# Moving the lambda sums and the scaling of the last norm's factors in a two-layer decoder trunk on one Trainium2 core

## The chip, the core and the metric

The kernel runs on one NeuronCore of a Trainium2 chip. TensorE (PE in the profile, with PEld for its weight loads) multiplies; VectorE (DVE), ScalarE (ACT) and GpSimd (POOL) work elementwise; SyncE (SP) and, for some transfers, POOL and ACT issue DMAs. Each engine takes its own instructions strictly in order, and engines wait for one another through semaphores. The metric is the device time of one launch in microseconds (us), the median of several runs.

## What is computed

The input is 256 tokens of width 1024, in float32. Two layers follow, and each has three blocks with a LayerNorm behind every one: a SwiGLU feed-forward block, a mixer (a gated spatial unit beside differential attention), and a second feed-forward block. Cut to what the change touches:

```python
def _swiglu(x, w1, w3, w2):
    return (jax.nn.silu(x @ w1) * (x @ w3)) @ w2          # w2: 2816 x 1024

    lam_full = (jnp.exp(jnp.sum(lf[0] * lf[1])) - jnp.exp(jnp.sum(lf[2] * lf[3])) + lam_init)
    a = p[:, :, 0] - lam * p[:, :, 1]                     # in the attention of each layer

    for l in range(DEPTH):
        h = _swiglu(x, ffn_w1[l, 0], ffn_w3[l, 0], ffn_w2[l, 0])
        x = _layernorm(ALPHA * x + 0.5 * h, ln_g[l, 0], ln_b[l, 0])
        h = _mixer(x, l, ...)
        x = _layernorm(ALPHA * x + h, ln_g[l, 1], ln_b[l, 1])
        h = _swiglu(x, ffn_w1[l, 1], ffn_w3[l, 1], ffn_w2[l, 1])
        x = _layernorm(ALPHA * x + 0.5 * h, ln_g[l, 2], ln_b[l, 2])
```

The lambda of a layer is one number made from 256 inputs. It is wanted first in the attention of the first mixer. `ln_g[1, 2]` are the factors of the very last norm.

## The kernel before

**Precision and pieces.** Every operand is split into a high part in a reduced float32 format and a low part that holds the rest, and each product is three matmuls: high by high, low by high, high by low. A weight comes from memory into a tile `raw` of 128x2048 (or two tiles `home` of 128x1024). ScalarE copies 128x1024 of it to `whi` (line 195 in `stream`, line 247 in `split`), VectorE subtracts that from the raw values into `wlo` (lines 197 and 249), and TensorE uses both. A `whi` with its `wlo` is called a piece here. There are 4 raw tiles, and 8 tiles each for high and low parts; a tile is filled again when its last reader is done.

**The product with w2.** `gemm_seven` (line 380) runs four times, once for each feed-forward block; these four stretches of the program are called the four w2 stages. It takes part of the product by seven block products in place of eight, and for that sums of weight blocks are made on the chip. `r1` holds block w11, `r2` is w12 and `r3` is w22, both in home tiles. `plus` (line 356, its addition is line 359) makes r1 + r2, and later in the same tile (r1 + r2) + r3; `pieces` (line 362) splits each sum, then r3, then r2. `product` (line 372) is 12 matmuls (line 376) with one such sum, and `between` (line 415) puts a piece of the ordinary product, 12 matmuls of line 405, between two of them. So TensorE's order in a w2 stage is fixed: product, piece, product, piece and so on. After each block product `Norm.fold` (line 606, its instruction is line 609) adds its result from PSUM to the tokens on VectorE. `gather` (line 350) lets POOL's DMA queue add a further weight block onto a tile in place. At the end a list `held` of seven pieces is multiplied for one half of the tokens and then for the other.

**What sets the order.** TensorE's order is as written. The other engines' order comes from a scheduler, which works by priority and by edges. `behind(ins)` makes an edge: what is issued inside comes after `ins` on its engine. While `line[2]` is set, `inline` notes the latest high split of ScalarE in `line[0]` and the latest operation of the split stream of VectorE in `line[1]`, so that splits and sums stay in one line. Small work is put beside the stream with `beside(task, delay)` (line 137): `beat(w)` (line 124) advances a clock as matmuls are written, a block product by 1 and a `between` by 1, and a task runs on when the clock has passed its time. A `yield 22` in a task hands back until the clock is 22 further.

**Lambda.** `setup` (line 543) is such a task. It is started in the first block, by the first row of a late piece of the first products. It loads the small constants through POOL's queue, yields 22, and then does: halving of a gate bias (`gbh`, line 556), two multiplications for lambda (`lampr`, line 560), scaling of `dgs` (line 570, one for each layer), the sums (`ls`, a reduction on VectorE, line 562), the Exp of the sums (ScalarE, line 563, with a load of the activation table ahead of it), and lambda itself (`neg_lam`, line 566, one for each layer). `lam` and `lampr` are tiles of a ring of four.

**The last norm.** `Norm.__init__` loads the factors g and the offsets b of its norm, spread over 128 partitions, with `bc_load` (a DMA of POOL's queue, line 576). For the last norm ScalarE multiplies g by -0.5 in place at once (line 595, `bc<-bc`). g is first read in `Norm.part` at line 620.

Of the kernel before, what the change touches and what calls it, by code (L numbers as in the profile page):

```python
# [16 lines left out]
AF = mybir.ActivationFunctionType  # L17
# [32 lines left out]
def lambda_init(layer):  # L50
    return 0.8 - 0.6 * math.exp(-0.3 * layer)
# [3 lines left out]
def trunk(ctx, tc, x, xT, w13a, w13b, w2, wb, wqk, wu, wg, wgr, wbr, wbrr, wo, gateb, gatebr, sgug, sgub, sguwT, sgubias, lam, diffg,  # L55
          lng, lnb, lngT, lnbT, cosT, sinT, out):
    nc = tc.nc
    V, A, G, PE = nc.vector, nc.scalar, nc.gpsimd, nc.tensor
# [15 lines left out]
    def name(s):  # L74
        serial[0] += 1
        return f"{s}_{serial[0]}"
# [24 lines left out]
    def s512(s, n=4):  # L101
        return tmp.tile([P, 512], F32, tag="side", name=name(s), bufs=n)

    def sm(s, n, dtype=F32, bufs=2):
        return small.tile([P, n], dtype, tag=f"{s}{n}", name=name(s), bufs=bufs)
# [31 lines left out]
    def beside(task, delay):  # L137
        tasks.append([clock[0] + delay, task])
# [9 lines left out]
    line = [None, None, False]  # L148
# [6 lines left out]
    def behind(ins):  # L155

        return tc.issue_after(ins) if ins is not None else nullcontext()
# [189 lines left out]
    def halved(v):  # L347
        return v if isinstance(v, list) else [v[:, o : o + HC] for o in range(0, CH, HC)]
# [194 lines left out]
    def setup(after):  # L543
        G.memset(mask[:, :P], 0.0)
        make_causal_mask(nc, mask[:, P:], NEG)
        lam_t = s512("lam").rearrange("p (l f d) -> p l f d", l=DEPTH, f=4)
        for dst, src in ((x_tok[0], x[:P, :]), (x_tok[1], x[P:, :]), (cos_t, cosT), (sin_t, sinT), (dgs, diffg),
                         (gbh, gateb), (ln_g, lngT), (ln_b, lnbT), (lam_t, lam.partition_broadcast(P))):
            first = dst
            while len(first.shape) > 2:  # L550
                first = first[:, 0]
            V.tensor_copy(first[:, :1], after)
            G.dma_start(dst, src)
        yield 22
        with behind(added[0]):
            V.tensor_scalar(out=gbh, in0=gbh, scalar1=0.5, scalar2=None, op0=ALU.mult)
        pr = s512("lampr").rearrange("p (l f d) -> p l f d", l=DEPTH, f=4)[:, :, :2]
        for j in range(2):
            with behind(added[0]):
                V.tensor_tensor(out=pr[:, :, j], in0=lam_t[:, :, 2 * j], in1=lam_t[:, :, 2 * j + 1], op=ALU.mult)  # L560
        ls = const.tile([P, DEPTH, 2], F32, name="ls")
        V.tensor_reduce(out=ls, in_=pr, op=ALU.add, axis=AX.X)
        A.activation(ls, ls, AF.Exp)
        for l in range(DEPTH):
            nl = const.tile([P, 1], F32, name=f"neg_lam{l}")
            V.tensor_scalar(out=nl, in0=ls[:, l, 1:2], scalar1=ls[:, l, 0:1], scalar2=-lambda_init(l),
                            op0=ALU.subtract, op1=ALU.add)
            neg_lam.append(nl)
            with behind(added[0]):
                V.tensor_scalar(out=dgs[:, l : l + 1], in0=dgs[:, l : l + 1], scalar1=1.0 - lambda_init(l),  # L570
                                scalar2=None, op0=ALU.mult)

    def bc_load(src, after):
        t = res.tile([P, D], F32, tag="bc", name=name("bc"), bufs=2)
        V.tensor_copy(t[:, :1], after)
        spread[0] = G.dma_start(t, src.partition_broadcast(P)).ins
        return t

    class Norm:
# [6 lines left out]
        def __init__(self, l, i, scale, eps, after, last=False):  # L586
            self.scale, self.eps, self.last, self.done, self.front = scale, eps, last, set(), i
            self.ends, self.xhi, self.xlo, self.rows = [None] * NT, {}, {}, {}
            self.gT, self.bT = (v[:, l, i] for v in (ln_g, ln_b))
            self.y = x_tok  # L590
            self.group = 256 if last else 512
            self.st = [sm("st", D // self.group * 6, bufs=2) for _ in range(NT)]
            self.g, self.b = bc_load(lng[l, i], after), bc_load(lnb[l, i], after)
            if last:
                A.activation(self.g, self.g, AF.Copy, scale=-0.5)
                self.minus = s512("minus")
                A.activation(self.minus[:, :P], ident, AF.Copy, scale=-1.0)
                self.eps_t = self.minus[:, 2 * P : 2 * P + 1]
                V.memset(self.eps_t, eps)
                with behind(silu[0]):  # L600
                    A.activation(sm("first", 1), mask[:, :1], AF.Sqrt)
            else:
                self.via = []
                self.x = [xs.tile([P, 4, 512], F32R, tag="x", name=name("x")) for _ in range(2)]

        def fold(self, t, c, ps, op, first):

            y = self.y[t][:, c * 512 : (c + 1) * 512]
            V.scalar_tensor_tensor(out=y, in0=y, scalar=self.scale if first else 1.0, in1=ps, op0=ALU.mult, op1=op)
# [137 lines left out]
    def ffn(l, f, i, norm, last=False):  # L747
# [14 lines left out]
        def front(n, wait):  # L762

            tiles = {}

            def gate_(t, ps):
                pool, tag = ((act, "val"), (res, "bc"))[n in (1, NB - 1)]
                p = pool.tile([P, D], F32, tag=tag, name=name("planes"), bufs=2).rearrange("p (w c) -> p w c", w=2)
                tiles[t] = p
                with behind(norm.xhi[1, 0] if norm and (n, t) == (0, 0) else None):  # L770
                    silu[0] = A.activation(p[:, 1], ps, AF.Silu).ins

            def done(t, ps):
                p = tiles[t]
                s = p[:, 1]
                added[0] = V.tensor_tensor(out=s, in0=s, in1=ps, op=ALU.mult).ins
                beside(turned(n, t, s, p[:, 0], wait[t]), 0)
                if norm is None and (n, t) == (2, 0):
                    beside(setup(s[:, :1]), 0)
            return gate_, done  # L780
# [546 lines left out]
```

## Time and profile before

| what | value |
|---|---|
| median of 3 runs | 1192.87 us (1192.68 to 1193.38) |
| the profiled execution: time | 1193.55 us |
| its span, first to last instruction | 1191.8 us |
| TensorE busy | 1182.0 us (99%), 5771 matmuls |
| VectorE busy | 1012.0 us (85%) |
| ScalarE busy | 827.5 us (69%) |
| POOL busy | 291.3 us (24%) |
| read from HBM | 249.10 MB |

The four w2 stages begin at 124.65, 537.51, 712.51 and 1124.03 us of the span. The rows shown below come from views of the one profiled execution. A row of a timeline gives the start, the duration, the engine, the line, the operation, what it writes and reads, and how many instructions of one kind were merged; in brackets stands how long the engine sat idle before it and what ended that. Starts and durations are in us. Line numbers are those of the kernel before.

### The profile page before, as it was taken

To read this page: it belongs to the slowest core of one execution; us is meant where nothing else is said; L and a number is where in the kernel's file an instruction comes from. 1 tells how busy PE (TensorE), PEld (TensorE's weight loads), DVE (VectorE), ACT (ScalarE), POOL (GpSimd) and SP (SyncE) were. 2 spreads that over 40 slices of the span, in tenths; PEclk is the share of its full clock that TensorE was granted. 3 is DMA by queue.
4 is the path that set the end of the run, shared out by engine and by line. 5 is a ranking of instruction groups with operands and counts; after the bars stand their busy time and mean duration, and the time that the engine had idled before them with its cause. 6 is when DMAs were issued, how large, how long until landed. Compare 5 with 4: busy or idle time off the path is not lost.

```text
span 1191.8 us, 16673 instructions
## 1 busy us (share of the span) xinstructions
PE 1182.0 (99%) x5771; PEld 993.3 (83%) x5771; DVE 1012.0 (85%) x1558; ACT 827.5 (69%) x1418; POOL 291.3 (24%) x356
## 2 busy tenths in 40 slices
PE   9999999999999999999999999999999999999998
PEld 7888888888888888888888888888888888888877
DVE  6889989888688989889899889788965989988885
ACT  6688658559955677876567876666788556679751
POOL 1111301247420220051020161004464012102500
PEclk9999999999999999999999999999999999999999
DMA  9869975758855658699667699586675764886971
GB/s 352 273 206 265 293 272 203 265 190 230 245 203 183 223 182 274 195 294 265 217 221 263 195 294 272 178 303 221 219 207 194 252 193 153 277 246 216 280 217 36
DMA packets 129797, 276.15 MB, mean 232 GB/s; under 512 B 89088, under 2 KB 90160, under 8 KB 105648
## 3 DMA queue, kind: packets, MB, share of 16 engines
q1 hardware_dynamic: 121968, 248.80, 62.9%
q0 software_dynamic: 7312, 25.76, 9.2%
q8 instruction: 45, 0.74, 0.2%
q10 hardware_dynamic: 432, 0.52, 0.1%
q14 instruction: 40, 0.33, 0.1%
HBM read 249.10 MB, written 1.05 MB: 210 GB/s over the span
## 4 chain that ended last, share of the span: by engine, by line
PE 96%; DVE 2%; DMA 1%; issue 1%; SPq 0%; ACT 0%; ACTq 0%; DVEq 0%
PE bank L283 46%; PE bank L295 15%; PE sbank L376 11%; PE bank L405 9%; PE bank L302 7%; PE sbank L405 3%; PE bank L516 1%; PE sbank L986 1%; DMA raw<-in_w13b 1%; PE bank L376 1%; PE sbank L1042 1%; PE sbank L1160 1%; DVE wlo L249 1%; PE sbank L1040 0%; DVE raw L359 0%
## 5 line engine op out<-in xcount | busy, mean ns | idle before, releaser
L197 DVE TENSOR_TENSOR wlo<-raw,whi 128x1024 fp32r<-128x1024 f32 (+1 forms) x374 | 414.1, 1132 | 56.1 <-ACT whi L195 43.1
L195 ACT ACTIVATE whi<-raw 128x1024 fp32r<-128x1024 f32 (+1 forms) x378 | 352.8, 959 | 131.2 <-PE bank L283 44.2
L283 PE MATMUL bank<-whi,x 128*128 128x512 f32 x1224 | 386.4, 390 | 0.0
L283 PEld LDWEIGHTS bank<-whi,x 128*128 128x128 f32 x1224 | 229.8, 188 | 47.6
L283 PE MATMUL bank<-wlo,x 128*128 128x512 f32 x612 | 238.2, 389 | 0.0
L295 PE MATMUL bank<-x,whi 128*128 128x512 f32 x640 | 153.3, 391 | 0.0
L295 PEld LDWEIGHTS bank<-x,whi 128*128 128x128 f32 x640 | 118.2, 188 | 23.8
L283 PEld LDWEIGHTS bank<-wlo,x 128*128 128x128 f32 x612 | 114.9, 188 | 23.4
L249 DVE TENSOR_TENSOR wlo<-raw,whi 128x1024 fp32r<-128x1024 f32 (+1 forms) x96 | 110.6, 1169 | 19.7 <-ACT whi L247 10.8
L247 ACT ACTIVATE whi<-raw 128x1024 fp32r<-128x1024 f32 (+1 forms) x96 | 92.6, 982 | 35.6 <-DVE raw L359 20.9
L229 POOL COPY seven<-seven 128x512 uint16<-128x512 uint16 x16 | 58.0, 3678 | 112.9 <-ACT whi L195 54.6
L302 PEld LDWEIGHTS bank<-x,wlo 128*128 128x128 f32 x640 | 81.4, 191 | 2.9
L302 PE MATMUL bank<-x,wlo 128*128 128x256 f32 x640 | 82.6, 283 | 0.0
L405 PE MATMUL bank<-whi,hhi 128*128 128x512 f32 (+1 forms) x182 | 68.2, 375 | 0.0
L405 PE MATMUL bank<-whi,hlo 128*128 128x512 f32 (+1 forms) x182 | 67.9, 373 | 0.0
L405 PE MATMUL bank<-wlo,hhi 128*128 128x512 f32 (+1 forms) x182 | 67.9, 373 | 0.0
L962 POOL TENSOR_TENSOR swap<-swap,sin_t 128x512 f32<-128x512 f32 x16 | 28.1, 1759 | 101.4 <-DMA swap<-z 84.6
L723 POOL COPY nvia<-ntwo 128x256 uint16<-128x256 uint16 x20 | 9.5, 520 | 157.5 <-DMA ntwo<-nvia 94.2
L303 ACT ACTIVATE r<-bank 128x256 f32<-128x256 f32 x96 | 34.8, 371 | 16.7 <-PE bank L302 16.7
L359 DVE TENSOR_TENSOR raw<-raw,home 128x1024 f32<-128x1024 f32 x32 | 38.6, 1216 | 4.3 <-DMA home<-in_w13b 4.3
L376 PE MATMUL sbank<-whi,xhs 128*128 128x512 f32 x128 | 42.0, 389 | 0.0
L405 PEld LDWEIGHTS bank<-whi,hlo 128*128 128x128 f32 x182 | 34.3, 188 | 6.1
(283 smaller groups left out, 2153.4 us busy)
## 6 DMA issues: line engine op xcount, KB each, us to landing
raw<-in_w13b SPq DMA_DIRECT2D x68, 1024.0 KB, 5.5
raw<-in_w SPq DMA_DIRECT2D x32, 1024.0 KB, 6.0
raw<-in_wb SPq DMA_DIRECT2D x16, 1024.0 KB, 5.3
raw<-in_wqk SPq DMA_DIRECT2D x16, 1024.0 KB, 5.7
home<-in_w13b SPq DMA_DIRECT2D x16, 512.0 KB, 6.1
raw<-in_w13a SPq DMA_DIRECT2D x8, 1024.0 KB, 4.8
home<-in_w SPq DMA_DIRECT2D x16, 512.0 KB, 5.1
raw<-in_wgr SPq DMA_DIRECT2D x8, 1024.0 KB, 5.3
```

What stands on the lines that cost most here:

```text
L195: inline(A, A.activation(h, r, AF.Copy).ins)
L197: low = eng.tensor_tensor(out=w, in0=r, in1=h.bitcast(F32), op=ALU.subtract).ins
L229: eng.tensor_copy(out=o, in_=i)
L247: a = A.activation(hi, src, AF.Copy).ins
L249: return a, eng.tensor_tensor(out=lo, in0=src, in1=hi.bitcast(F32), op=ALU.subtract).ins
L283: PE.matmul(ps, xx, w, start=start and n == 0, stop=stop and n == 2)
L295: PE.matmul(b[-1], hi[:, k * P : (k + 1) * P], xc(k), start=k == 0, stop=False)
L302: PE.matmul(b[n][:, :T], lo[:, k * P : (k + 1) * P], xc(k)[:, :T], start=False, stop=k == KT - 1)
L303: emptied[0] = A.activation(r[:, s], b[n][:, T:], AF.Copy, scale=scale).ins
L359: inline(V, V.tensor_tensor(out=v, in0=v, in1=m, op=ALU.add).ins)
L376: PE.matmul(ps, x[o](k), y, start=start and k == n == 0, stop=stop and k == 3 and n == 2, skip_group_check=True)
L405: PE.matmul(q[c][t][:, :n] if o == 0 else more[:, :n], x(k, t), y, start=k == 8 and m == 0 and (c, t) != (1, 0), stop=k == FT - 1 and m == ...
```

## The change

```diff
@@ -551,7 +551,7 @@
-        yield 22
+        yield 33
         with behind(added[0]):
             V.tensor_scalar(out=gbh, in0=gbh, scalar1=0.5, scalar2=None, op0=ALU.mult)
@@ -592,7 +592,7 @@
             if last:
-                A.activation(self.g, self.g, AF.Copy, scale=-0.5)
+                beside(self.halved(), 9)
                 self.minus = s512("minus")
@@ -602,6 +602,11 @@
+        def halved(self):
+            with behind(line[0]):
+                A.activation(self.g, self.g, AF.Copy, scale=-0.5)
+            yield 0
```

No instruction is added or removed, and TensorE, POOL and SyncE keep their order. Line numbers behind the change are 5 higher (609 becomes 614). Three places move.

VectorE in the first w2 stage, where the third block sum is made (`raw<-raw,home` is the addition of r3, `xtok<-xtok,sbank` a fold). Before:

```order
L197 TENSOR_TENSOR wlo_1360<-raw_1353,whi_1359 128x1024
L556 TENSOR_SCALAR gbh<-gbh 128x32
L560 TENSOR_TENSOR lampr_1370<-lam_791 128x2x64 x2
L570 TENSOR_SCALAR dgs<-dgs 128x1 x2
L562 TENSOR_REDUCE ls<-lampr_1370 128x4
L359 TENSOR_TENSOR raw_1233<-raw_1233,home_1316 128x1024
L609 TENSOR_SCALAR xtok_144<-xtok_144,sbank_1230 128x512
L566 TENSOR_SCALAR neg_lam_1376<-ls 128x1
L566 TENSOR_SCALAR neg_lam_1379<-ls 128x1
L359 TENSOR_TENSOR raw_1233<-raw_1233,home_1317 128x1024
L249 TENSOR_TENSOR wlo_1391<-raw_1233,whi_1390 128x1024
L249 TENSOR_TENSOR wlo_1395<-raw_1233,whi_1394 128x1024
```

And with the change:

```order
L197 TENSOR_TENSOR wlo_1360<-raw_1353,whi_1359 128x1024
L359 TENSOR_TENSOR raw_1233<-raw_1233,home_1316 128x1024
L359 TENSOR_TENSOR raw_1233<-raw_1233,home_1317 128x1024
L614 TENSOR_SCALAR xtok_144<-xtok_144,sbank_1230 128x512
L249 TENSOR_TENSOR wlo_1378<-raw_1233,whi_1377 128x1024
L249 TENSOR_TENSOR wlo_1382<-raw_1233,whi_1381 128x1024
```

The eight small instructions have left, and the fold has gone from between the two additions to behind them. ScalarE's table load and Exp have left the same place.

ScalarE at the end of the first w2 stage, with the change (`raw_1550` and `raw_1560` are the last weights of this stage, `lhi` and `raw_1732` belong to the mixer's first product):

```order
L195 ACTIVATE whi_1546<-raw_1540 128x1024
L195 ACTIVATE whi_1552<-raw_1550 128x1024
L563 ACT_TABLE_LOAD
L563 ACTIVATE ls<-ls 128x4
L195 ACTIVATE whi_1556<-raw_1550 128x1024
L195 ACTIVATE lhi_1734<-raw_1732 128x512
L195 ACTIVATE whi_1562<-raw_1560 128x1024
```

The table load and the Exp stand here now, ahead of the sixth of the seven held pieces. On VectorE the gate bias, the products, the scalings and the sums stand between the fourth and the fifth held piece, and the two lambdas around the next statistics.

ScalarE in the last w2 stage (`bc` are the norm's factors, `raw_11074` or `raw_11073` is the block sum, the homes are r3). Before:

```order
L195 ACTIVATE whi_11200<-raw_11194 128x1024
L595 ACTIVATE bc_11057<-bc_11057 128x1024
L247 ACTIVATE whi_11218<-raw_11074 128x1024
L247 ACTIVATE whi_11222<-raw_11074 128x1024
L247 ACTIVATE whi_11253<-home_11157 128x1024
L247 ACTIVATE whi_11257<-home_11158 128x1024
L195 ACTIVATE whi_11275<-raw_11273 128x1024
```

And with the change:

```order
L195 ACTIVATE whi_11199<-raw_11193 128x1024
L247 ACTIVATE whi_11217<-raw_11073 128x1024
L247 ACTIVATE whi_11221<-raw_11073 128x1024
L247 ACTIVATE whi_11252<-home_11156 128x1024
L247 ACTIVATE whi_11256<-home_11157 128x1024
L608 ACTIVATE bc_11057<-bc_11057 128x1024
L195 ACTIVATE whi_11275<-raw_11273 128x1024
```

The scaling has moved behind the four high splits of the third block sum and of r3. VectorE's order in this stage is the same as before.

## The prediction

> **What bounds the kernel now.** I read the page's busy shares first, then the list of what TensorE waited for over the whole span.
>
> ```profile
> PE 1182.0 (99%) x5771; PEld 993.3 (83%) x5771; DVE 1012.0 (85%) x1558; ACT 827.5 (69%) x1418; POOL 291.3 (24%) x356
> PE sbank L376 <- DVE wlo L249: 1.8, 2, 1.0
> PE bank L516 <- ACT whi L247: 1.4, 2, 0.8
> PE sbank L528 <- DVE warm L524: 1.0, 1, 1.0
> PE sbank L376 <- ACT whi L247: 0.8, 1, 0.8
> PE sbank L659 <- ACT minus L657: 0.8, 1, 0.8
> ```
>
> TensorE is the bound from end to end. A row of the list gives the sum, the count and the longest wait in us. Lines 516 and 528 belong to the start, line 659 to the tail behind the last product; in between TensorE waits three times, always at line 376, the block products. Matmul ends are modelled, so these waits are too short; the true loss comes from comparing equal work. The four w2 stages run the same matmuls from their first block product to the last one, and the windows view gives each stretch:
>
> ```profile
> 124.65:161.38 36.73, 35.71 (x158) 29.21 (x157) 36.15 (x49) 24.59 (x29) 4.64 (x6) 1.00 0.96 296
> 537.51:572.93 35.42, 35.42 (x159) 29.32 (x158) 34.12 (x40) 22.77 (x26) 4.52 (x6) 1.00 0.96 276
> 712.51:747.92 35.41, 35.41 (x159) 29.31 (x158) 34.10 (x40) 22.77 (x26) 4.50 (x6) 1.00 0.92 270
> 1124.03:1161.93 37.90, 36.27 (x159) 29.13 (x157) 34.00 (x41) 24.61 (x30) 4.50 (x6) 1.00 0.78 222
> ```
>
> After the length come the busy times of PE, PEld, DVE, ACT and POOL, then the granted clock, 1.00 in all four, and the DMA share. The two middle stages have no loss: busy equals length. The first is 36.73 - 35.41 = **1.32 us** longer, the last 37.90 - 35.41 = **2.49 us**. The change touches exactly these two. A matmul in the stream follows the one before by 35.41 / 156 = 0.227 us (13 groups of 12; the view counts a few more that an edge cuts).
>
> **First stage: what goes, and what then ends last.** VectorE, ScalarE and TensorE around the stall:
>
> ```profile
> 134.81 2.35 DVE L197 TENSOR_TENSOR wlo<-raw,whi 128x1024 fp32r<-128x1024 f32 x2
> 137.08 0.17 DVE L556 TENSOR_SCALAR gbh<-gbh 128x32 f32<-128x32 f32 x1
> ...
> 138.02 1.22 DVE L359 TENSOR_TENSOR raw<-raw,home 128x1024 f32<-128x1024 f32 x1
> 139.15 0.68 DVE L609 SCALAR_TENSOR_TENSOR xtok<-xtok,sbank 128x512 f32<-128x512 f32 x1
> 139.75 0.33 DVE L566 TENSOR_SCALAR neg_lam<-ls 128x1 f32<-128x1 f32 x2
> 140.00 1.21 DVE L359 TENSOR_TENSOR raw<-raw,home 128x1024 f32<-128x1024 f32 x1
> 141.13 2.49 DVE L249 TENSOR_TENSOR wlo<-raw,whi 128x1024 fp32r<-128x1024 f32 x2
> ...
> 134.97 1.28 ACT L563 ACT_TABLE_LOAD   x1
> 138.14 0.21 ACT L563 ACTIVATE ls<-ls 128x4 f32<-128x4 f32 x1 [1.89 <-DVE ls L562]
> 139.33 1.06 ACT L247 ACTIVATE whi<-raw 128x1024 fp32r<-128x1024 f32 x1 [0.98 <-DVE raw L359]
> ...
> 141.00 0.39 PE L376 MATMUL sbank<-whi,sum 128*128 128x512 f32 x1
> 142.40 0.50 PE L376 MATMUL sbank<-wlo,sum 128*128 128x512 f32 x1 [1.02 <-DVE wlo L249]
> ```
>
> VectorE runs without a gap: one instruction starts as the last ends. TensorE wanted the first low part of the sum at 141.00 + 0.23 = 141.23 and got it at 142.40, 0.05 after its end (141.13 + 1.22, the length of one such operation, = 142.35). The lambda work costs this queue 138.02 - 137.08 = 0.94 and 140.00 - 139.75 = 0.25, together 1.19. Without it: additions at 137.08 and 138.21 (they follow each other by 1.13), fold at 139.35, first subtraction at 139.35 + 0.60 = 139.95, done at 141.17, taken at 141.22. That is when it is wanted, to 0.01. The second low part comes 1.13 later, at 142.35; it is wanted seven matmuls into the product, at 142.6. ScalarE's first copy starts 0.09 after the first addition ends, 138.30 + 0.09 = 138.39, and is done at 139.45, ahead of VectorE. The homes that are added must have landed 0.94 us sooner than they were needed before:
>
> ```profile
> L171 SPq DMA_DIRECT2D home<-in_w x4: 327/426/566, 116.1 to 124.8; - x4
> DMA to landing us min/median/max: 4.9/7.5/9.1
> ```
>
> The last of their transfers is issued at 124.8 and the longest takes 9.1, so they are there by 133.9.
>
> So the stall's bounds are 0 (kept whole) and 1.32 (gone); I take **1.3**, since the worked-out arrival equals the wanted one, and the middle stages show the same queue keeping up. What is late next? VectorE stays fully booked, but 1.1 us earlier against a TensorE that is 1.3 earlier; its next due date is r3's first low part, ready two subtractions after the first one starts, at 139.95 + 2 x 1.13 + 1.22 = 143.4, and wanted 25 matmuls after 141.0, at 146.7, so it holds.
>
> **The same work, later.** VectorE's 1.19 us now stand among the held pieces, and the table load and Exp (1.28 + 0.21) ahead of the sixth. Here are that copy before, the first time ScalarE has nothing left to prepare, and the start of the product with the held pieces:
>
> ```profile
> 161.58 1.06 ACT L195 ACTIVATE whi<-raw 128x1024 fp32r<-128x1024 f32 x1 [1.66 <-PE bank L405]
> 175.18 1.15 ACT L195 ACTIVATE whi<-raw 128x512 fp32r<-128x512 f32 x2 [5.85 <-PE bank L405]
> 164.10 0.39 PE L405 MATMUL sbank<-whi,hhi 128*128 128x512 f32 x1
> ```
>
> The sixth copy waited 1.66 us for TensorE to release its tile; load and Exp, 1.49, fit into that. Were the cover gone, the piece is wanted at 164.10 + 5 x 6 x 0.227 = 170.9, 8 us after its copy ended, and ScalarE idles another 5.85 before the next stage's pieces. VectorE is ahead as far. Cost: **0**, and below zero nothing, since no work disappears. The ring tile of the lambda inputs is held some 22 us longer, but is free before the norm at 175 needs one. Lambda is used only in the mixer.
>
> **Last stage.** ScalarE, VectorE and TensorE:
>
> ```profile
> 1131.14 1.99 ACT L195 ACTIVATE whi<-raw 128x1024 fp32r<-128x1024 f32 x2
> 1139.27 1.06 ACT L595 ACTIVATE bc<-bc 128x1024 f32<-128x1024 f32 x1 [6.13 <-DMA bc<-in_lng]
> 1140.23 1.99 ACT L247 ACTIVATE whi<-raw 128x1024 fp32r<-128x1024 f32 x2
> 1135.27 2.35 DVE L359 TENSOR_TENSOR raw<-raw,home 128x1024 f32<-128x1024 f32 x2
> 1141.31 1.22 DVE L249 TENSOR_TENSOR wlo<-raw,whi 128x1024 fp32r<-128x1024 f32 x1 [3.69 <-ACT whi L247]
> 1140.15 0.39 PE L405 MATMUL bank<-whi,hlo 128*128 128x512 f32 x1
> 1141.33 0.49 PE L376 MATMUL sbank<-whi,sum 128*128 128x512 f32 x1 [0.79 <-ACT whi L247]
> ```
>
> The sum was ready at 1137.6, but ScalarE stood 6.13 us before the scaling, whose factors had not landed, with the sum's copies queued behind it. With the scaling behind four copies, the first copy starts after the first addition, 1135.27 + 1.22 + 0.09 = 1136.6, ends at 1137.6, and the subtraction ends at 1138.9; TensorE wants the copy at 1140.4 and the low part at 1140.6. The second low part follows a fold, at 1140.6, against 1142.0. Everything is over 1 us early, so the whole **2.49** goes, between bounds of 0 and 2.49. The scaling now starts when the four copies are done, about 1136.6 + 4 x 1.0 = 1140.6, after the landing at 1139.3: no wait. Behind it stands the next piece's copy, now at 1141.7; before, it came after the same four copies from 1140.23, at 1144. The factors are read some 25 us on.
>
> **Sum.** -1.3 + 0 - 2.49 = -3.8 us: the profiled span goes from 1191.8 to 1188.0, its execution from 1193.55 to 1189.75. That execution lies 0.7 above the median of the runs, 1192.87; against the median I predict **1189.1 us**, 0.32% less. The tail after the last matmul is unchanged.
>
> **Rivals.** (1) *The fold takes the stall's place.* It now precedes both subtractions, and arrival meets demand without margin; a bank released late or a slower semaphore would keep up to half or all of the 1.32. Against it: its block product ends at 138.4, 0.9 before its turn. Time 1189.8 to 1190.4. (2) *Given back downstream*: TensorE runs early and meets a weight that has not landed. For it, a DMA share of 0.96 in the first stage; against it, the middle stages, at the same 0.96, lose nothing, and no DMA is in the list of waits. Time up to 1192.9, no measurable change. (3) *Slower: the scaling still blocks ScalarE, with more behind it.* If the factors land late, the copies of the next piece wait.
>
> ```profile
> 1131.15 0.86 POOL L576 DMA_DIRECT2D bc<-in_lng  x1
> DMA to landing us min/median/max: 5.2/7.7/9.3
> ```
>
> The issue here, and the landings of all six such loads. The next piece is wanted at 1151.05 - 2.49 = 1148.6; scaling, copy and semaphore take 2.2, so a landing up to 1146.3, 15 us after issue, costs nothing. From there each us is one on the path; beyond 19 us the kernel is slower than before, beyond 21 measurably. The longest seen is 9.3, in the first stage, with VectorE busy 36.15 of 36.73.
>
> The Trainium skill (SBUF — State Buffer, Who interferes with whom) speaks for rival 3: a DMA of GpSimd's queue needs its descriptors written through a port pair that VectorE can lock, and VectorE would no longer idle here from 1137.6. By that rule the landing would slip until VectorE runs dry behind the scaling, which by the rows above is near 1143, and so to about 1144.6, still under 1146.3: the sum stays, the margin shrinks from 7 us to under 2. The 9.3 with VectorE busy disagrees with a lock that long.
>
> **How the numbers follow.** Forecast 0.82; rival 1 0.10; rival 2 0.05; rival 3 0.03 (1195.3 and up, were it to happen). The runs differ by 0.7, so the low end is 1189.1 - 0.5 = 1188.6; the high end is rival 1's 1190.4 with 0.2 added, 1190.6. About 0.2% (2.4 us) is what a measurement tells from no change. Faster by more: the forecast and most of rival 1, 0.89; within it 0.08; slower 0.03.
>
> **What would show it.** Right: the first and last w2 stages at 35.4 us like the middle ones, no wait at line 376, the scaling without idle time ahead of it, the Exp followed by a copy that still waits for TensorE. Wrong: a wait at the first sum's low part in the first stage (rival 1), a matmul waiting for a load later on (rival 2), idle time before the scaling of over 5 us (rival 3).

## The result, and the profile after

| | before | after |
|---|---|---|
| median of 9 runs each, side by side | 1193.19 us (1192.30 to 1196.01) | 1189.86 us (1189.26 to 1191.88) |
| ratio | | 0.9971, 95% interval 0.9961 to 0.9981 |
| profiled execution: time, span | 1193.55, 1191.8 us | 1189.92, 1188.2 us |

The kernel is 0.29% faster: by the interval 2.3 to 4.7 us. The prediction said 1189.1 us and -3.8 us.

The page of the changed kernel first, then the whole list of what TensorE waited for:

```profile
PE 1180.8 (99%) x5771; PEld 993.6 (84%) x5771; DVE 1010.2 (85%) x1558; ACT 828.5 (70%) x1418; POOL 297.3 (25%) x356
```

```profile
PE bank L516 <- ACT whi L247: 1.7, 1, 1.7
PE sbank L528 <- DVE warm L524: 1.0, 1, 1.0
PE sbank L664 <- ACT minus L662: 0.8, 1, 0.8
```

The three waits at line 376 are gone. What is left belongs to the start (516, 528) and to the tail (664, before 659).

To size the gain I cut the span at marks that both kernels have: from a w2 stage's first block product (the first matmul of line 376) to the first matmul of what follows it (line 283, after the last stage the tail's first matmul). Here are the first and the last of these stretches before:

```profile
124.65:183.64 58.99, 57.97 (x259) 47.62 (x257) 54.11 (x83) 38.16 (x54) 5.66 (x8) 1.00 0.81 259
1124.03:1184.24 60.21, 58.58 (x296) 49.34 (x295) 46.87 (x66) 27.04 (x33) 5.02 (x7) 1.00 0.52 149
```

And all four of the changed kernel, in the windows view; behind the stretch and its length stand the busy times of PE, PEld, DVE, ACT and POOL, then the clock, the DMA share and GB/s:

```profile
124.85:182.63 57.78, 57.78 (x258) 47.62 (x257) 53.66 (x83) 38.05 (x54) 5.73 (x8) 1.00 0.81 263
536.53:594.18 57.65, 57.65 (x259) 47.71 (x257) 51.86 (x74) 36.15 (x51) 5.95 (x8) 1.00 0.79 243
711.50:769.14 57.64, 57.64 (x258) 47.72 (x257) 51.87 (x74) 35.75 (x49) 4.51 (x6) 1.00 0.77 244
1122.92:1180.62 57.70, 57.70 (x296) 49.49 (x295) 46.77 (x66) 27.32 (x33) 5.03 (x7) 1.00 0.53 157
```

In all four TensorE's busy time now equals the length, although the first is still 0.13 us longer than the second: busy time alone does not show that rest. The first stage is 58.99 - 57.78 = **1.21 us** shorter, the last 60.21 - 57.70 = **2.51 us**. The middle ones are as before. The kernel's start is 0.20 longer (124.85 against 124.65), and the stretch between the third and the last stage 0.10 shorter: 0.20 - 1.21 - 0.10 - 2.51 = -3.62, which is the tail's first matmul at 1180.62 instead of 1184.24. So the gain lies in the two stages that the change touches.

**First stage.** The timeline of VectorE, ScalarE, TensorE and its weight loads (PEld) where the stall was:

```profile
137.29 2.35 DVE L359 TENSOR_TENSOR raw<-raw,home 128x1024 f32<-128x1024 f32 x2
139.56 0.68 DVE L614 SCALAR_TENSOR_TENSOR xtok<-xtok,sbank 128x512 f32<-128x512 f32 x1
140.16 2.36 DVE L249 TENSOR_TENSOR wlo<-raw,whi 128x1024 fp32r<-128x1024 f32 x2
138.60 2.20 ACT L247 ACTIVATE whi<-raw 128x1024 fp32r<-128x1024 f32 x2 [3.44 <-DVE raw L359]
141.43 0.50 PE L376 MATMUL sbank<-wlo,sum 128*128 128x512 f32 x1
141.43 0.19 PEld L376 LDWEIGHTS sbank<-wlo,sum 128*128 128x128 f32 x1 [0.27 <-DVE wlo L249]
```

VectorE still has no gap in these rows, and the subtraction starts 140.16 - 124.85 = 15.31 us behind the stage's first matmul, where it was 141.13 - 124.65 = 16.48. A short wait has stayed, but not in the list for TensorE's matmuls: it sits on the weight load, 0.27 us. So of the signs that the prediction named for being right, the missing wait at line 376 came true by that list only, and the first stage is not quite like the middle ones.

**The moved work.** ScalarE at the end of the first stage, then VectorE at the first sum that needs the finished product:

```profile
157.86 1.07 ACT L195 ACTIVATE whi<-raw 128x1024 fp32r<-128x1024 f32 x1 [1.66 <-PE bank L405]
158.94 1.28 ACT L563 ACT_TABLE_LOAD   x1
160.24 0.20 ACT L563 ACTIVATE ls<-ls 128x4 f32<-128x4 f32 x1
160.64 1.06 ACT L195 ACTIVATE whi<-raw 128x1024 fp32r<-128x1024 f32 x1 [0.20 <-PE bank L405]
172.82 0.69 DVE L619 SCALAR_TENSOR_TENSOR xtok<-xtok,sbank 128x512 f32<-128x512 f32 x1 [3.17 <-PE sbank L405]
```

Table load and Exp take 1.28 + 0.20 us, and the copy behind them still waits 0.20 for TensorE. VectorE still idles 3.17 us before the stage's last sum.

**Last stage.** POOL's issue of the factors' load, and ScalarE:

```profile
1130.04 0.86 POOL L576 DMA_DIRECT2D bc<-in_lng  x1
1135.47 2.20 ACT L247 ACTIVATE whi<-raw 128x1024 fp32r<-128x1024 f32 x2 [3.44 <-DVE raw L359]
1139.47 1.05 ACT L608 ACTIVATE bc<-bc 128x1024 f32<-128x1024 f32 x1
```

The copies of the sum now wait for VectorE's addition, as in the other stages. The scaling (line 608) has no idle time ahead of it: the load was issued at 1130.04, 9.4 us earlier, and had landed.

### The profile page after: what moved, and what is told of

Same layout as the page of the kernel before. It is cut to its first block, busy times and chain, and to the rows that moved or that the text cites. A ratio compares the mean times of both kernels' runs of the same rounds, so it can differ in the third digit from the quotient of the medians.

```text
span 1188.2 us, 16675 instructions
## 1 busy us (share of the span) xinstructions
PE 1180.8 (99%) x5771; PEld 993.6 (84%) x5771; DVE 1010.2 (85%) x1558; ACT 828.5 (70%) x1418; POOL 297.3 (25%) x356
## 3 DMA queue, kind: packets, MB, share of 16 engines
HBM read 249.10 MB, written 1.05 MB: 211 GB/s over the span
## 4 chain that ended last, share of the span: by engine, by line
PE 99%; DMA 1%; DVE 0%; ACT 0%; SPq 0%; issue 0%; ACTq 0%
PE bank L283 46%; PE bank L295 15%; PE sbank L376 12%; PE bank L405 10%; PE bank L302 8%; PE sbank L405 3%; PE bank L516 2%; PE sbank L991 1%; PE bank L376 1%; PE sbank L1047 1%; PE sbank L1165 1%; DMA raw<-in_w13b 1%; PE sbank L1045 0%; PE sbank L685 0%; PE sbank L664 0%; SPq L494 0%
## 5 line engine op out<-in xcount | busy, mean ns | idle before, releaser
L229 POOL COPY seven<-seven 128x512 uint16<-128x512 uint16 x16 | 63.7, 4041 | 108.4 <-ACT whi L195 54.6
L303 ACT ACTIVATE r<-bank 128x256 f32<-128x256 f32 x96 | 34.8, 372 | 16.6 <-PE bank L302 16.5
```

The source lines that it names most:

```text
L229: eng.tensor_copy(out=o, in_=i)
L303: emptied[0] = A.activation(r[:, s], b[n][:, T:], AF.Copy, scale=scale).ins
```

## The experiments

The theory: in the first stage VectorE's queue ran without a gap, so each us of lambda work in it was lost by TensorE; in the last stage ScalarE's wait for the factors' landing was the stall; the moved work is hidden at its new place. The main rivals: ScalarE's table load or the time of the scaling itself was (part of) the loss, or the new place has a price. Since the start of a kernel alone differs by up to 2.6 us from profile to profile (the first mark lies between 123.94 and 126.51), single changes are judged by the stretches between the marks; the reference is 57.78 / 57.70 us (first / last stage) with the change and 58.99 / 60.21 before. Line numbers behind an edit are some lines higher.

**Each edit alone.** The lambda work:

```diff
-        yield 22
+        yield 33
```

> The kernel before with the sums for lambda late and the scaling where it was. My theory: the two edits act in two places and add up. First w2 stage 57.8 us (58.99 before, 57.78 with both edits), last stage unchanged at 60.2 us; span 1.2 us less than before, some 1190.6; ratio 0.999. Rival, that the last norm's load or scaling also profits from the earlier finish of stage one, or that VectorE's lambda work was not the first stage's stall: the first stage stays at 59.0, or the last one changes by more than 0.2 us.

The scaling alone is the rest of the change's diff:

```diff
-                A.activation(self.g, self.g, AF.Copy, scale=-0.5)
+                beside(self.halved(), 9)
```

> The kernel before with the scaling of the last norm's factors late and the sums for lambda where they were. My theory: first w2 stage unchanged at 59.0 us, last one 57.7 us (60.21 before); span 2.5 us less than before, some 1189.3; ratio 0.998. Together with the run of the other edit the gains add up to the 3.6 us of both. Rival: the gains overlap or one needs the other, so that the two do not add up to within 0.3 us.

| | first stage | last stage | ratio to before, 95% interval |
|---|---|---|---|
| lambda alone | 57.94 | 59.49 | 0.9993, 0.9984 to 1.0002 |
| scaling alone | 58.99 | 57.70 | 0.9986, 0.9977 to 0.9995 |
| both | 57.78 | 57.70 | 0.9971, 0.9961 to 0.9981 |

Each edit mends its own stage, to 0.16 us of what both give, and the gains add up: 1.05 + 2.51 = 3.56 us by the stages, where both edits have 3.72. By the times it is 0.07 and 0.14% against 0.29%, which the intervals allow; the first of these is not told from no change, so the gain of the lambda edit rests on the stages. With the lambda work alone the last stage is 0.72 us shorter than expected, although nothing in it was edited. POOL and ScalarE there:

```profile
1129.82 0.86 POOL L576 DMA_DIRECT2D bc<-in_lng  x1
1137.24 1.06 ACT L595 ACTIVATE bc<-bc 128x1024 f32<-128x1024 f32 x1 [5.43 <-DMA bc<-in_lng]
```

From issue to scaling it is 7.42 us here, where the first profile of before had 1139.27 - 1131.15 = 8.12. The transfer took 0.70 less, and the stage is 0.72 shorter. Is the size of the stall set by how long this one transfer takes? Two more profiles of the kernel before, unedited, were to tell.

> The kernel before once more, for how far its last stage's stall differs from one execution to the next. My theory: the stall is the landing time of the factors, counted from the issue to the scaling's start, less 5.6 us (8.12 us and a loss of 2.51 us in the first profile of it; 7.42 and 1.79 us in the run with the lambda work alone), and the first stage's loss is how far the low part's start lies behind 15.16 us from the stage's first matmul. Rival, that the loss is a fixed 2.5 us.

> As the run beside it: a third profile of the kernel before. Last stage 57.70 us plus the factors' landing time less 5.6 us; first stage 57.65 us plus what the low part's start lies behind 15.16 us.

The first of them, then the second (windows view of the first and last stage):

```profile
125.10:184.08 58.98, 57.96 (x259) 47.63 (x257) 54.16 (x83) 38.05 (x54) 5.66 (x8) 1.00 0.81 255
1124.43:1184.29 59.86, 58.57 (x297) 49.33 (x295) 46.87 (x66) 27.03 (x33) 5.04 (x7) 1.00 0.52 150
```

```profile
124.49:183.58 59.09, 57.96 (x258) 47.63 (x257) 54.13 (x83) 38.27 (x54) 5.71 (x9) 1.00 0.80 255
1123.85:1183.21 59.36, 58.54 (x296) 49.34 (x295) 46.88 (x66) 27.05 (x33) 5.03 (x7) 1.00 0.53 151
```

The issue and the scaling in the same two profiles:

```profile
1131.54 0.86 POOL L576 DMA_DIRECT2D bc<-in_lng  x1
1139.33 1.06 ACT L595 ACTIVATE bc<-bc 128x1024 f32<-128x1024 f32 x1 [5.80 <-DMA bc<-in_lng]
```

```profile
1130.96 0.86 POOL L576 DMA_DIRECT2D bc<-in_lng  x1
1138.22 1.06 ACT L595 ACTIVATE bc<-bc 128x1024 f32<-128x1024 f32 x1 [5.27 <-DMA bc<-in_lng]
```

| old place of the scaling | issue to scaling | last stage less 57.70 | difference |
|---|---|---|---|
| first profile of before | 8.12 | 2.51 | 5.61 |
| before again, 1 | 7.79 | 2.16 | 5.63 |
| lambda alone | 7.42 | 1.79 | 5.63 |
| before again, 2 | 7.26 | 1.66 | 5.60 |

The loss is the time from issue to scaling less 5.6 us in all four. (The scaling starts 0.16 us after the landing that the trace gives.) The rival of a fixed 2.5 us falls. The first profile happened to have the longest of the four; the mean loss is 2.03 us.

**ScalarE's half of the lambda work put back.** An Exp of one column, and with it the table load, stands again ahead of the third sum's copies:

```diff
-        yield 33
+        yield 22
+        with behind(line[0]):
+            A.activation(sm("first", 1), mask[:, :1], AF.Exp)
+        yield 11
```

> The changed kernel, with an Exp of one column, and so the load of its table, put back on ScalarE at the place where the old kernel had it, ahead of the copies of the third sum of weights; VectorE's lambda work stays late. It splits the first stage's gain between the engines. My theory: the stall came from VectorE alone, since ScalarE's copies wait for VectorE's sum (3.44 us idle there after the change) and the 1.5 us of load and Exp fit in it: first stage 57.8 us as with the change. Rival, that the table load on ScalarE was the stall, or a part of it: first stage 58.5 to 59.3 us.

ScalarE in this kernel:

```profile
134.75 1.28 ACT L556 ACT_TABLE_LOAD   x1
136.04 0.20 ACT L556 ACTIVATE first<-mask 128x1 f32<-128x1 f32 x1
138.17 2.20 ACT L247 ACTIVATE whi<-raw 128x1024 fp32r<-128x1024 f32 x2 [1.93 <-PE sbank L376]
```

The first stage took 57.94 us, the same as with the lambda edit alone (the 0.16 above 57.78 are VectorE's, see the table below). The copies still wait 1.93 us behind load and Exp, so ScalarE was no part of the stall.

**VectorE's half put back**, by a stand-in of two reductions:

```diff
-        yield 33
+        yield 22
+        ls = const.tile([P, DEPTH, 2], F32, name="ls")
+        for _ in range(2):
+            with behind(line[1]):
+                V.tensor_reduce(out=ls, in_=lam_t[:, :, :2], op=ALU.add, axis=AX.X)
+        yield 11
```

> The changed kernel, with two more reductions on VectorE (128 x 256 to 128 x 4, about 0.33 to 0.41 us each) ahead of the two additions of the third block sum, where the lambda work stood; nothing is put back on ScalarE. My theory: VectorE's queue ahead of the block sum sets the first stage, so each 0.1 us there is lost by TensorE: 0.66 to 0.82 us more, first stage 58.4 to 58.6 us, with a wait at line 376 (here shifted by some lines) of about 0.8 us. Rival, that it was ScalarE: first stage 57.8 us. The lambda work at the end of the stage stands some instructions apart here, which by my theory costs nothing.

```profile
138.81 0.41 DVE L558 TENSOR_REDUCE ls<-lam 128x4 f32<-128x256 f32 x1
139.13 1.22 DVE L359 TENSOR_TENSOR raw<-raw,home 128x1024 f32<-128x1024 f32 x1
140.27 0.41 DVE L558 TENSOR_REDUCE ls<-lam 128x4 f32<-128x256 f32 x1
140.60 1.22 DVE L359 TENSOR_TENSOR raw<-raw,home 128x1024 f32<-128x1024 f32 x1
```

The reductions take 0.32 and 0.33 of the queue. The first stage took 58.30 us, 0.52 above the changed kernel and below the expected 0.66 to 0.82. The first subtraction of the sum also started only 0.50 later, 15.81 instead of 15.31 us behind the first matmul, since the queue ahead of the reductions ran 0.14 sooner: two subtractions around the start of the stage took 1.63 and 1.21 us here, 1.22 and 1.76 in the profile of the change. The last section shows what lengthens them. TensorE lost what the subtraction was late.

The first stages together give the rule; only the run with six reductions ahead of the Exp (below) is left out, since its stage loses again at its end. x is the start of the sum's first subtraction on VectorE, counted from the stage's first matmul:

| kernel | x | first stage | 57.65 + (x - 15.16) |
|---|---|---|---|
| fold behind (below) | 14.85 | 57.64 | 57.65, no loss |
| six reductions late, ScalarE's order kept (below) | 15.30 | 57.75 | 57.79 |
| small copies early (below) | 15.30 | 57.78 | 57.79 |
| the change | 15.31 | 57.78 | 57.80 |
| lambda alone; Exp early | 15.42 | 57.94 | 57.91 |
| scaling sooner (below) | 15.68 | 58.16 | 58.17 |
| two reductions early | 15.81 | 58.30 | 58.30 |
| scaling alone; before; before again, 1 | 16.47, 16.48, 16.48 | 58.99, 58.99, 58.98 | 58.96 to 58.97 |
| before again, 2 | 16.60 | 59.09 | 59.09 |

From 15.16 us on, TensorE loses what VectorE's queue is late, one for one. 15.16 was read off the rows at hand before the last three runs (the two repeats of before, and six reductions with ScalarE's order kept), so that the line fits is one constant; that its slope is 1 over 1.4 us is the finding, and the three later runs fall on it to 0.04 us. The change brings x from 16.5 to 15.3 or 15.7, so it leaves 0.1 to 0.5 us.

**Taking the rest away.** The fold stood between the additions and the subtractions; it goes behind both:

```diff
-        ln.fold(1, 1, bz, ALU.add, True)
...
-        product(bx, sums[1], pieces(plus(r1, r3)), False, False)
+        parts = pieces(plus(r1, r3))
+        with behind(line[1]):
+            ln.fold(1, 1, bz, ALU.add, True)
+        product(bx, sums[1], parts, False, False)
```

> The changed kernel, with the fold of a sum into the tokens (0.6 us of VectorE) put behind both low parts of the third block sum in all four w2 stages, where it stood between the additions and the low parts. My theory: in the first stage the low parts then start 0.6 us sooner against TensorE, 14.7 us behind the stage's first matmul where 15.2 is early enough, and the 0.1 to 0.3 us that the change has left there go: first stage 57.65 us like the middle ones; the others as they are, unless the sbank that the fold frees is wanted sooner. Rival, that what is left is no wait for VectorE: first stage 57.8 to 57.9. Whole kernel at most 0.3 us faster, which the times can't tell from none.

VectorE, TensorE and its weight loads in this kernel:

```profile
139.25 2.36 DVE L249 TENSOR_TENSOR wlo<-raw,whi 128x1024 fp32r<-128x1024 f32 x2
140.75 0.39 PE L376 MATMUL sbank<-whi,sum 128*128 128x512 f32 x1
140.75 0.19 PEld L376 LDWEIGHTS sbank<-wlo,sum 128*128 128x128 f32 x1
140.97 0.39 PE L376 MATMUL sbank<-wlo,sum 128*128 128x512 f32 x1
```

The first stage took 57.64 us; the other three are 57.65, 57.64 and 57.70. The rest of the stall was VectorE's as well. Timed: median 1189.72 us of 7 runs, ratio to before 0.9973, 0.9961 to 0.9984. The times can't tell it from the change (0.9971); by the profiles it is 0.1 to 0.5 us better.

**The scaling's own time.** Four small copies of ScalarE that need no load stand at the scaling's old place; the scaling stays late:

```diff
             if last:
+                beside(self.stand(), 6)
                 beside(self.halved(), 9)
...
+        def stand(self):
+            for _ in range(4):
+                with behind(line[0]):
+                    A.activation(self.minus[:, 3 * P :], ident, AF.Copy, scale=-0.5)
+            yield 0
```

> The changed kernel, with four small copies by ScalarE (128 x 128 each, about 1.06 us in all, as long as the scaling) at the scaling's old place right ahead of the copies of the third sum of weights in the last w2 stage; they need nothing that is loaded there, the scaling itself stays late. My theory: the old stall was the wait for the load, not the 1.06 us of ScalarE's time: last w2 stage 57.7 us as with the change. Rival, that ScalarE's time at that place was a part of the loss: last stage 58.2 to 58.8 us.

ScalarE in this kernel:

```profile
1131.00 1.32 ACT L610 ACTIVATE minus<-ident 128x128 f32<-128x128 f32 x4
1134.54 2.20 ACT L247 ACTIVATE whi<-raw 128x1024 fp32r<-128x1024 f32 x2 [2.22 <-DVE raw L359]
```

The copies took 1.32 us, and the last stage 57.70 us; ScalarE still idled 2.22 us behind them. So ScalarE's time at this place costs nothing by itself. It counted in the old kernel only because it stood behind the wait: the sum's copies came after the landing and the 1.06 us of the scaling, and both are in the 5.6 us above.

**The scaling two steps sooner**, where it does wait:

```diff
-                beside(self.halved(), 9)
+                beside(self.halved(), 7)
```

> The changed kernel, with the scaling of the factors two steps sooner on ScalarE: behind the third sum's two copies, but ahead of the two copies of the block that follows. My theory: it waits there for its load, about 0.5 to 1.5 us, but TensorE wants the two copies behind it some 5 us later: last w2 stage 57.7 us, no wait at line 376. Rival, that any wait for the load on ScalarE in this stage costs TensorE: last stage 58.2 us or more.

```profile
1130.19 0.86 POOL L576 DMA_DIRECT2D bc<-in_lng  x1
1138.49 1.06 ACT L608 ACTIVATE bc<-bc 128x1024 f32<-128x1024 f32 x1 [0.68 <-DMA bc<-in_lng]
```

ScalarE waits 0.68 us for the load, and the last stage takes 57.70 us all the same: what stands behind it was wanted later. It is not the wait but what is queued behind it that costs. (There is a wait of 0.2 us at line 376 in this profile, but in the first stage, which took 58.16 us; see the table.)

**Is there a price at the new place?** Six more reductions beside the lambda work, ahead of the Exp:

```diff
         V.tensor_reduce(out=ls, in_=pr, op=ALU.add, axis=AX.X)
+        for _ in range(6):
+            V.tensor_reduce(out=ls, in_=pr, op=ALU.add, axis=AX.X)
         A.activation(ls, ls, AF.Exp)
```

> The changed kernel, with six more reductions on VectorE (128 x 256 to 128 x 4, about 0.41 us each, 2.5 us in all) beside the lambda work at its new place, behind the end of the first w2 stage's product; the Exp waits for them too. It tests the zero that the prediction gave the moved work. My theory: VectorE idles over 3 us there waiting for TensorE, so even 2.5 us more cost nothing: span to within 0.3 us of the changed kernel's beyond what the kernel's start and the first stage's low parts differ, from the first w2 stage's end to the second one's start as with the change (353.8 us). Rival, that the late place has no cover left: up to 2.5 us more in that stretch.

The theory missed: the first stage took 59.42 us, and from its end to the second stage's start it was 355.14 us instead of 353.90, together 2.9 us lost. ScalarE, VectorE and TensorE in this kernel:

```profile
164.96 0.63 ACT L195 ACTIVATE lhi<-raw 128x512 fp32r<-128x512 f32 x1 [6.50 <-DMA raw<-in_wb]
166.57 1.23 DVE L197 TENSOR_TENSOR wlo<-raw,whi 128x1024 fp32r<-128x1024 f32 x1 [2.93 <-ACT whi L195]
175.79 0.68 DVE L621 SCALAR_TENSOR_TENSOR xtok<-xtok,sbank 128x512 f32<-128x512 f32 x1
180.64 0.63 PE L687 MATMUL sbank<-ident,xtok 128*128 128x128 f32 x4 [1.52 <-issue]
```

With the Exp later, the scheduler had put a copy for the mixer's first product (`lhi`) ahead of the last held pieces, and ScalarE stood 6.50 us before its load. VectorE stood 2.93 us behind that, had no idle time left before the sum (line 621, 175.79 - 124.42 = 51.37 us behind the stage's first matmul instead of 172.82 - 124.85 = 47.97), and the norm that follows reached TensorE late. That reading makes the order the culprit; to test it, the reductions go behind the lambda work, where ScalarE's order stays that of the change:

```diff
+        for _ in range(6):
+            V.tensor_reduce(out=ls, in_=pr, op=ALU.add, axis=AX.X)
```

> The changed kernel, with six more reductions on VectorE (0.33 us each at the engine's pace, 2.0 us in all) behind the lambda work at its new place; unlike the run with six reductions ahead of the Exp, ScalarE's order stays as with the change. That run lost 3 us, about 1.6 at the stage's end and 1.4 behind it. My theory: it lost them because ScalarE's queue was put in another order and stood 6.50 us for a load, which took VectorE's cover; the 2.0 us alone fit in the 3.17 us that VectorE idles ahead of the last sum. First stage 57.6 to 57.9 us apart from the delay of its low parts, from there to the second stage 353.8 us. Rival, that VectorE's added work itself was the loss: 1 to 2 us more between the first stage's end and the second stage's start.

```profile
172.03 0.69 DVE L621 SCALAR_TENSOR_TENSOR xtok<-xtok,sbank 128x512 f32<-128x512 f32 x1 [0.53 <-PE sbank L405]
```

The first stage took 57.75 us, and 353.89 us lie between it and the second: no loss. VectorE's idle time before the sum fell from 3.17 to 0.53 us. So the work alone is not what cost the other run; that its order did remains the reading, which no run had by itself. The lambda work is free where it is, but the cover is finite: 2.0 us more nearly use it up, and a stall of ScalarE ahead of it does not fit.

## Why the prediction was right, and where not

- **Two stages, and only these.** Right. The losses against the middle stages were read as 1.32 and 2.49; 1.21 and 2.51 went.
- **First stage, -1.3.** The mechanism was right: VectorE's queue alone (work put back there made the subtraction 0.50 later and the stage 0.52 longer), ScalarE's load and Exp for nothing (57.94 with and without them). The step that was mis-sized is the one that said when TensorE wants the first low part, "141.00 + 0.23 = 141.23", and found the arrival equal to it "to 0.01". The arrival was right: the subtraction was worked out for 139.95, 15.30 behind the first matmul, and came at 15.31. The demand was too late by 0.14: it is at 15.16, because the part is wanted by its weight load, and that runs ahead of the matmul: in the kernel with the fold behind, load at 140.75, as the matmul before starts, its own matmul at 140.97. (The load leads by 0.22 and the demand moved by 0.14; the 0.08 between was not traced.) The term measured -1.21 in this pair of profiles. By all profiles of each arrangement, 59.01 (four) against 57.89 (six: the change, lambda alone, Exp early, small copies early, scaling sooner, six reductions with ScalarE's order kept), it is -1.1. The Trainium skill (TensorE: Matmul & The Clock Gate, Step-by-step: what each phase is for) says that weight loads are pulled ahead of matmuls still under way; these rows agree, with 0.22 us.
- **Rival 1, the fold takes the stall's place.** The place was right to a tenth: the stall kept 0.13 of the 1.32 in the first profile, up to 0.51 in another, and moving the fold took it away. Its two reasons did not show: no bank and no semaphore held the fold up, it followed the additions without idle time. The forecast named the place and held the margin for zero; it was slightly negative.
- **The moved work, 0.** Right, and shown with 2.0 us on top. The cover that the prediction named for ScalarE, the 1.66 us wait, shows as the 0.20 that is left of it.
- **Last stage, -2.49.** Right in place and mechanism. Its size was that of one execution: the loss followed the landing time, 1.66 to 2.51 us in four profiles, mean 2.03. That 2.49 and the first pair's 2.51 agree confirms the size only for that execution, since both are read from the same profile of before; that the forecast took the longest of the four landings was chance. The sum of the means, -1.1 - 2.0 = -3.1 us, and the measured ratio (-2.3 to -4.7 us) agree; the predicted -3.8 lay in the interval, but above the mean, since both terms were taken at the upper end of what the executions show.
- **Rival 2, given back downstream.** Did not happen: between the first stage and the second 353.90 us against 353.88 before.
- **Rival 3, the scaling still blocks.** Did not happen; even where it waits, 0.68 us, nothing is lost. The rule quoted for it, from the Trainium skill (SBUF — State Buffer, Who interferes with whom), was taken to delay the landing until VectorE runs dry. In the nine profiles with the late scaling VectorE idled at most 0.06 us between issue and landing, and the factors landed 6.9 to 8.2 us after the issue; in the four with the old order, where VectorE ran dry 0.6 to 1.5 us before the landing, it was 7.1 to 8.0. No such delay is seen. The same section's list of operations that take the shared ports does not count a TENSOR_TENSOR among those that held up a DMA, and that is most of what VectorE ran there: the rule was applied more widely than the Trainium skill does.
- **The time.** 1189.86 us against 1189.1: the runs of before beside it had 1193.19 where the forecast started from 1192.87, which makes 0.3 of the 0.8; the rest, 0.4, lies within what the smaller means of the two terms give (3.1 instead of 3.8).

## What to carry to other kernels

Cut a profile at marks that repeat and compare equal work: the stages without a loss tell what the others lose, where the list of waits shows only a part. Where an engine's queue runs without a gap up to the point where TensorE wants its result, small work in it costs its full length, and the same work beside an idle time costs nothing, until that idle time is used up. A stall that ends with a transfer's landing is as long as the landing happens to be: look at several executions before sizing it, and move what waits for the transfer behind what TensorE wants next, since a wait costs only by what is queued behind it.

## What the runs showed of the hardware that was not expected

- A short wait for a weight can show on the weight load alone: in the changed kernel the list of TensorE's waits has nothing at line 376, while PEld has 0.27 us there and the stage is 0.13 us too long. The longer wait of before shows on both, 1.44 us on the load and 1.02 on the matmul, and neither is the loss of 1.32.
- A table load and the first function behind it follow each other directly: Exp at 160.24, 0.02 us after the load's end (158.94 + 1.28); 136.04 against 136.03 in the kernel with the Exp early. A switch cost ScalarE 1.5 us with its Exp, no more.
- The factors' load of the last stage took 6.9 to 8.2 us from issue to landing in the thirteen profiles; in the five where ScalarE waited for it, it was 7.26 to 8.30 from issue to use.
- What one subtraction on VectorE takes differs from place to place and from profile to profile, and where the queue has no gap that arrives at TensorE: one just ahead of the first stage took 1.22 us with the change (first fence) and 1.35 with the lambda edit alone (second fence), where x is 0.11 larger. The traces show with what it goes together, a copy on POOL (line 229). In the first fence it began 0.03 us after the subtraction; in the second it began before, at 121.40, and the subtraction ended 1.02 us behind that copy's end.

```profile
122.23 1.22 DVE L249 TENSOR_TENSOR wlo<-raw,whi 128x1024 fp32r<-128x1024 f32 x1 [1.63 <-issue]
122.26 1.83 POOL L229 COPY planes<-planes 128x512 uint16<-128x512 uint16 x1 [0.35 <-DMA planes<-planes]
124.00 0.78 POOL L229 COPY planes<-planes 128x512 uint16<-128x512 uint16 x1
124.03 1.76 DVE L249 TENSOR_TENSOR wlo<-raw,whi 128x1024 fp32r<-128x1024 f32 x1
```

```profile
121.40 0.77 POOL L229 COPY planes<-planes 128x512 uint16<-128x512 uint16 x1
121.85 1.35 DVE L249 TENSOR_TENSOR wlo<-raw,whi 128x1024 fp32r<-128x1024 f32 x1 [1.67 <-issue]
```

In the thirteen profiles every one of the 406 subtractions of a 128x1024 raw tile (of 4888) that took more than 1.27 us began while a copy or product of POOL, begun before it, was still running, and ended 1.01 to 1.09 us behind that instruction's end; the others took 1.19 to 1.27. Not every such meeting lengthens a subtraction, and no run moved POOL's work, so this is read from the traces and not tried. With the change a second subtraction, at 124.03, took 1.76 us in this way, 0.54 too long, and the rest of the first stage's stall was 0.13. By the rule for x above, a first stage without that would lose nothing, which no run tried.
